# First half's attention in a hybrid encoder layer: vector work moved between a step's low halves and its normalisation, ScalarE's part moved to the step's head, one weight unit per step

## The chip, the cores and the metric

One core of one Trainium2 chip runs the whole layer as one program. The metric is the device time of one execution in microseconds (us). The engines are TensorE (PE in the profile; PEld is its loading of weights), VectorE (DVE), ScalarE (ACT), GpSimd (POOL) and the queue that issues most loads (SP). Each works through its own list of instructions in order, and they wait for one another through semaphores.

## The reference, cut to what matters

One layer over 1024 positions of width 1024. The change lies in branch B of the token mixer, a windowed attention with 8 query heads and 2 key/value heads of width 64, in blocks of 128 positions:

```python
q = rmsnorm(q.reshape(b, s, N_HEADS, HEAD_DIM), q_gain)
k = rmsnorm(k.reshape(b, s, N_KV_HEADS, HEAD_DIM), k_gain)
v = v.reshape(b, s, N_KV_HEADS, HEAD_DIM)
# each block of 128 queries sees its own block of keys and one on either side
logits = einsum('bnqkgd,bnskd->bnkgqs', qb, kb) * HEAD_DIM ** -0.5
logits = where(valid, logits - slope * distance, -1e30)
probs = softmax(concatenate([logits, sink_logit]))[..., :-1]
out = einsum('bnkgqs,bnskd->bnqkgd', probs, vb)
```

Beside it stand branch A (a gated mixing of 128 positions, with u and v from the same input projection), the sigmoid gates of both branches, an output projection and a gated feed-forward layer. All is float32; a product of two matrices is made of three passes over operands that are split into a high half and a low half (high x high, high x low, low x high).

## The kernel before, in words

The 1024 positions are done in two halves of 512 (`half(0)`, `half(1)`); each half has four query blocks i and two key/value heads kv. **A step** is one pair (i, kv), `work[s]`, so a half has steps 0 to 7. Step s does, in program order:

- `q_step(s)`, the *scores*: for four heads two matmuls each into a PSUM bank `at`, and on VectorE a custom instruction that adds the bias and takes the maximum (`lb`, `nmx`; ISA in an order's row, CUSTOM_DVE_ANT_0 in a profile's).
- `transposed(st)`: the probabilities of step s-1 (`lb`) are transposed on TensorE, block by block, and split: ScalarE casts the high half (`pH`), VectorE subtracts for the low half (`pL`).
- `exps`: VectorE makes `es`, ScalarE the exponentials of step s (`lb`) and of the sink (`es`).
- two *fillers*: 12 matmuls of another product (v of branch A first, then the gates), which give TensorE something to do.
- `normalise`: VectorE adds the sink, takes the reciprocal (`den`) and scales the four `lb`.
- `values`: TensorE multiplies the probabilities of step s-1 by `vt`; ScalarE copies half of the result (`xs`), VectorE adds the other half (`xs`), ScalarE casts it (`mid`), GpSimd subtracts for its low half.
- `beside(s)`, in the first half only: what the later steps need and was not ready before the loop: the split of the values (`v_split`, tiles `vt`), the split of the last query block (`q_halves(3)`, tiles `t`), its transposes (`q_turn(3)`), the norm and scale of the last key block (`k_norm(4)` with `kms` and `krs`; `k_put(4)` with `kd`) and its transposes (`turn_k`, into `kbuf`).
- one more filler.

In this stretch `in_order[0]` is true, so every engine's list has the order of the program text. There are four banks `at`, taken in turn: the scores take four, the transposes of a three-block step three, the values one. The scores of a step therefore take over banks that VectorE's `pL` and `xs` of the step before let go, and the first transposes of a step take over the bank of its first scores, which VectorE's custom instruction (`nmx`) lets go.

A *weight unit* is 128x1024 of a weight matrix: a load into `raw`, ScalarE's cast `wh`, and the subtraction `wl`, which `prepare` gives to GpSimd. `prepare_due` at a step's start makes as many units as the fillers have used up; before the change `beside(1)` makes one more, ahead of need.

Almost every instruction has line 76 in the profile (a helper records it), so groups are told apart by their tiles.

Of the kernel before, what the change touches and what calls it, by code (L numbers as in the profile page):

```python
# [38 lines left out]
def kernel(  # L39
# [709 lines left out]
    def half(hf):  # L749
# [323 lines left out]
        def begin_unit():  # L1073
            r = raw_unit(srcs.pop(0))
            h, l = (wpool.tile([P, UNIT], F32R, tag=x, name=nm(x)) for x in ("wh", "wl"))
            A.copy(h, r)
            units.append((h, l))
            return lambda: V.tensor_tensor(l, r, h.bitcast(F32), op=ALU.subtract)
# [109 lines left out]
        if hf == 0:  # L1188
# [92 lines left out]
            vgs = []  # L1281
            vr = sm(NT, "vr")

            def beside(s):
                if s == 0:
                    q_turn(2)
                    kv_tile(4, 0)
                    turn_k(2, 2)
                    kv_tile(4, 1)
                    k_evict(4)  # L1290
                    lows.append(begin_unit())
                elif s == 1:
                    q_halves(3)
                    v_split(2)
                    k_norm(4)
                    prepare()
                elif s == 2:
                    v_split(3)
                    q_turn(3)
                elif s == 3:  # L1300
                    v_split(4)
                    k_put(4)
                elif s == 4:
                    turn_k(4, 1)

            lows = []
        else:
            kraw, banks = [], []
            for b in range(3):
# [59 lines left out]
        for s in range(nw):  # L1369
            if s:  # L1370
                prepare_due()
                sc = q_step(s)
                if hf == 0 and s == 1:
                    lows.pop()()
                pts = transposed(st)
                den = exps(*sc, work[s][1])
            fill(FA if hf or s else 0)
            if hf == 0 and 0 < s < 7:
                x_square(s + 1)
            if hf == 0 and s == 7:  # L1380
                x_rstd()
            if hf == 0 and s == 5:
                load(silu_d, silu_c)
            normalise(sc[0], sc[2], den)
            if s == 0:
                end_unit()
            st = sc[0]
            if s == nw - 1:
                for vg in vgs:
                    act[0] = after(A.activation(vg, vg, AF.Gelu_apprx_tanh), act[0])  # L1390
                for t, vg in enumerate(vgs[:3]):
                    V.tensor_tensor_reduce(
                        out=stream("hs"), in0=vg, in1=vg, op0=ALU.mult, op1=ALU.add,
                        scale=1.0, scalar=0.0, accum_out=vr[:, t : t + 1])
            if s:
                i, kv = work[s - 1]
                values(base + i, koff, kv, pts, vts, i, oH, oL)
            if s == nw - 1:
                A.activation(stream("hs"), vgs[3], AF.Square, accum_out=vr[:, 3:])
                for vg in vgs[:2]:  # L1400
                    V.tensor_tensor(vg, vg, vgain, op=ALU.mult)
                V.tensor_scalar(vr, vr, 1.0 / GW, EPS, op0=ALU.mult, op1=ALU.add)
                G.tensor_tensor(vr, vr, nhalf[:, :NT], op=ALU.pow)
            if hf == 0:
                beside(s)
            fill(FB)
        pts = transposed(st)
        fill(FC)
# [55 lines left out]
            copies = {}  # L1464
        if hf == 0:
            ada_load()
            x_load(0)
            x_load(1)
            jobs.extend((k, lambda k=k: x_mod(k)) for k in range(KT))
# [12 lines left out]
        for d in range(KT):  # L1482
# [14 lines left out]
            for br, t in ((1, (oH, oL)), (0, (gH, gL))):  # L1497
# [4 lines left out]
                for k in range(4):  # L1502
                    kc = slice(br * Q + k * P, br * Q + (k + 1) * P)
                    mm3(pb, (wab[d][0][:, kc], wab[d][1][:, kc]), (t[0][:, k, :], t[1][:, k, :]),
                        k == 0, k == 3)
                if hf + d == 0 and br:
                    x_spread()
                if d < 2:
                    sg = gates.pop(0)
                    V.scalar_tensor_tensor(out=sg, in0=sg, scalar=1.0, in1=pb, op0=ALU.add,  # L1510
# [819 lines left out]
```

## Time and profile before

| | |
|---|---|
| median of 3 runs | 1236.48 us (1235.93 to 1240.13) |
| the profiled execution | 1236.45 us, of which the span of its instructions is 1234.6 us |
| TensorE (PE) busy | 1218.2 us, 99% of the span |
| VectorE (DVE) busy | 913.4 us, 74% |
| ScalarE (ACT) busy | 582.5 us, 47% |
| GpSimd (POOL) busy | 183.8 us, 15% |
| mean granted clock of TensorE | 0.997 |
| steps 1 to 7 of the first half | about 82.8 to 152.6 us of the span |

A timeline's row has the start, the time busy, the engine, the operation, the written and the read tiles with their sizes, the count of instructions put together, and in brackets the idle time before with what ended it. A row of windows has a stretch of the span, then the busy time of each engine in it, then the clock that TensorE was granted (1.00 is full), the busy share of the DMA engines, and GB/s. TensorE is pipelined and the ends of its matmuls are modelled, so the starts of rows are the better ruler.

### The profile page before, as it was taken

What the parts mean: (1) busy time and instruction counts of PE and PEld (TensorE: products, weight loads), DVE (VectorE), ACT (ScalarE), POOL (GpSimd) and SP (SyncE); (2) the same over time, 40 slices, a digit from 0 to 9 for tenths busy, and PEclk for the clock granted to TensorE, in tenths of its full rate; (3) what the DMA queues carried; (4) which work ended last, traced back from release to release, by engine and by line L of the source; (5) the groups of instructions that cost most, each with busy time, mean ns of one, the idle gap of its engine ahead of it and who ended that gap; (6) DMA issues with size and microseconds to landing.
All of it is one profiled execution on the core that took longest, in us unless ns stands there. A gap on an engine that the chain in (4) does not pass through costs nothing.

```text
span 1234.6 us, 15745 instructions
## 1 busy us (share of the span) xinstructions
PE 1218.2 (99%) x5680; PEld 1014.8 (82%) x5680; DVE 913.4 (74%) x1542; ACT 582.5 (47%) x954; POOL 183.8 (15%) x231
## 2 busy tenths in 40 slices
PE   8997999999999999999999999999999999999998
PEld 7886888888888887888888888888888888888887
DVE  9887786388898799877798666766766666666746
ACT  5586864267886333534553323333333334434342
POOL 0134331023342001222100000010000000010001
PEclk9998999999999999999999999999999999999999
DMA  9812249421147557877613445554555459996542
GB/s 346 322 52 69 78 148 323 161 86 53 59 140 257 176 180 255 284 269 243 234 35 120 140 151 204 187 208 155 212 194 188 170 187 372 337 351 235 188 171 102
DMA packets 78621, 235.76 MB, mean 191 GB/s; under 512 B 9344, under 2 KB 9680, under 8 KB 73552
## 3 DMA queue, kind: packets, MB, share of 16 engines
q1 hardware_dynamic: 56112, 141.43, 32.9%
q0 software_dynamic: 18976, 87.04, 19.8%
q10 hardware_dynamic: 3456, 6.29, 1.4%
q8 instruction: 44, 0.72, 0.2%
q14 instruction: 33, 0.27, 0.1%
HBM read 177.06 MB, written 57.67 MB: 190 GB/s over the span
## 4 chain that ended last, share of the span: by engine, by line
PE 90%; ACT 4%; DVE 3%; DMA 2%; issue 1%; SPq 0%; POOL 0%; DVEq 0%; ACTq 0%; POOLq 0%
PE at L76 46%; PE mm L76 45%; ACT lb L76 1%; ACT mid L76 1%; DVE lb L76 1%; ACT pH L76 1%; DMA mid<-in_xo_dram 1%; DMA raw<-in_w_ga_dram 0%; DVE xs L76 0%; DMA raw<-in_w_ada_dram 0%; DVE vt L76 0%; ACT wh L76 0%; SPq L137 0%; ACT t L76 0%; DVE t L76 0%
## 5 line engine op out<-in xcount | busy, mean ns | idle before, releaser
L76 ACT CAST wh<-raw 128x1024 fp32r<-128x1024 f32 (+1 forms) x156 | 161.7, 1039 | 142.2 <-PE mm L76 34.6
L76 DVE TENSOR_TENSOR wl<-raw,wh 128x1024 fp32r<-128x1024 f32 (+1 forms) x147 | 171.1, 1169 | 75.1 <-ACT wh L76 69.6
L76 PE MATMUL mm<-mid,wh 128*128 128x512 f32 x696 | 214.9, 390 | 0.0
L76 PEld LDWEIGHTS mm<-mid,wh 128*128 128x128 f32 x696 | 130.5, 188 | 27.0 <-DVE mid L76 0.2
L76 PE MATMUL at<-j,wh 128*128 128x512 f32 x464 | 142.9, 389 | 0.0
L76 PE MATMUL mm<-mid,wl 128*128 128x512 f32 x348 | 135.9, 390 | 0.6 <-DVE wl L76 0.6
L76 PE MATMUL mm<-wh,h 128*128 128x512 f32 x320 | 104.4, 398 | 0.5 <-ACT h L76 0.5
L76 PEld LDWEIGHTS at<-j,wh 128*128 128x128 f32 x464 | 87.1, 188 | 18.0
L76 DVE TENSOR_TENSOR wl<-ws,wh 128x1024 fp32r<-128x1024 f32 (+1 forms) x53 | 59.1, 1114 | 54.0 <-ACT wh L76 54.0
L76 PE MATMUL at<-j,wl 128*128 128x512 f32 x232 | 90.2, 389 | 0.0
L76 PE MATMUL mm<-j,wh 128*128 128x512 f32 x288 | 89.0, 390 | 0.0
L76 PE MATMUL mm<-h,wh 128*128 128x512 f32 x272 | 84.5, 392 | 0.0
L76 PE MATMUL at<-h,wh 128*128 128x512 f32 x272 | 84.3, 391 | 0.0
L76 PEld LDWEIGHTS mm<-mid,wl 128*128 128x128 f32 x348 | 65.3, 188 | 15.5 <-DVE wl L76 2.1
L76 ACT CAST wh<-ws 128x1024 fp32r<-128x1024 f32 (+1 forms) x53 | 50.9, 961 | 53.3 <-DVE ws L76 35.4
L76 PEld LDWEIGHTS mm<-wh,h 128*128 128x128 f32 x320 | 60.1, 190 | 12.8 <-ACT h L76 0.9
L76 PEld LDWEIGHTS mm<-j,wh 128*128 128x128 f32 x288 | 53.9, 188 | 11.1
L76 PEld LDWEIGHTS at<-h,wh 128*128 128x128 f32 x272 | 50.7, 188 | 11.2 <-DVE mid L76 0.8
L76 DVE TENSOR_TENSOR ol<-raw,oh 128x1024 fp32r<-128x1024 f32 x30 | 36.6, 1224 | 30.7 <-ACT oh L76 29.1
L76 PEld LDWEIGHTS mm<-h,wh 128*128 128x128 f32 x272 | 50.6, 188 | 10.3
L76 PE MATMUL mm<-wl,h 128*128 128x512 f32 x160 | 58.8, 392 | 0.0
L76 PE MATMUL mm<-j,wl 128*128 128x512 f32 x144 | 56.2, 390 | 0.0
(325 smaller groups left out, 2591.7 us busy)
## 6 DMA issues: line engine op xcount, KB each, us to landing
raw<-in_w_gate_dram SPq DMA_DIRECT2D x28, 512.0 KB, 5.2
tA<-hid POOLq DMA_DIRECT2D x11, 1024.0 KB, 5.0
tB<-hid POOLq DMA_DIRECT2D x11, 1024.0 KB, 5.5
wo<-in_w_out_dram POOLq DMA_DIRECT2D x22, 512.0 KB, 6.8
wS<-wo POOLq DMA_DIRECT2D x11, 1024.0 KB, 5.1
raw<-wS SPq DMA_DIRECT2D x44, 256.0 KB, 3.1
raw<-tB SPq DMA_DIRECT2D x44, 256.0 KB, 4.2
raw<-in_w_out_dram SPq DMA_DIRECT2D x33, 256.0 KB, 5.4
```

The source lines that it names most:

```text
L76: ins = f(*args, **kw)
```

## The change

`beside` is cut down to what TensorE does, and moves ahead of `values`. Three new places take the rest. `head(s)` stands behind the scores: ScalarE's casts of the values (`v_halves`) and of the query block (`q_begin`) are issued there, and VectorE's subtractions that belong to them are put on a list. `inside(s)` stands between `exps` and `normalise`: it runs that list (`run_lows`), and makes `k_norm(4)` in step 3 and `k_put(4)` in step 4. `head(5)` makes the weight unit that `beside(1)` made, so that each step from 2 on makes one. The query split moves from step 1 to step 3, its transposes from step 2 to step 4, and the transposes of the key block from step 4 to step 5. Apart from the attention, `x_spread` (four matmuls and a ScalarE copy that spread the next half's norm over the partitions) moves from between the first two output products to ahead of the loads of the next half's input.

```diff
+            def v_halves(t):
+                vts[t] = halo_v[t] = vt = attp.tile([P, 2, P], F32R, tag="vt", name=nm("vt"), bufs=5)
+                src = kraw(t)[:, P:]
+                for h in range(NKV):
+                    A.copy(vt[:, h, h * HD : (h + 1) * HD], src[:, h * HD : (h + 1) * HD])
+                    lows.append(lambda h=h: V.tensor_tensor(
+                        vt[:, h, (1 - h) * HD : (2 - h) * HD], src[:, h * HD : (h + 1) * HD],
+                        vt[:, h, h * HD : (h + 1) * HD].bitcast(F32), op=ALU.subtract))
+
+            def q_begin(t):
+                q3 = qraw[:, t, :].rearrange("p (h d) -> p h d", d=HD)
+                q0[t] = [tmp(F32R) for _ in range(2)]
+                for g in range(2):
+                    src = q3[:, g * 4 : g * 4 + 4, :]
+                    q4 = q0[t][g].rearrange("p (h a d) -> p h a d", a=2, d=HD)
+                    A.copy(q4[:, :, 0, :], src)
+                    lows.append(lambda q4=q4, src=src: V.tensor_tensor(
+                        q4[:, :, 1, :], src, q4[:, :, 0, :].bitcast(F32), op=ALU.subtract))
+
+            def head(s):
+                if s == 1:
+                    lows.append(begun.pop())
+                elif s == 2:
+                    v_halves(2)
+                    v_halves(3)
+                elif s == 3:
+                    q_begin(3)
+                elif s == 4:
+                    v_halves(4)
+                elif s == 5:
+                    prepare()
+
+            def run_lows():
+                while lows:
+                    lows.pop(0)()
+
+            def inside(s):
+                run_lows()
+                if s == 3:
+                    k_norm(4)
+                elif s == 4:
+                    k_put(4)
+
             def beside(s):
                 if s == 0:
                     q_turn(2)
...
-                    lows.append(begin_unit())
-                elif s == 1:
-                    q_halves(3)
-                    v_split(2)
-                    k_norm(4)
-                    prepare()
-                elif s == 2:
-                    v_split(3)
+                    begun.append(begin_unit())
+                elif s == 4:
                     q_turn(3)
-                elif s == 3:
-                    v_split(4)
-                    k_put(4)
-                elif s == 4:
+                elif s == 5:
                     turn_k(4, 1)
...
                 sc = q_step(s)
-                if hf == 0 and s == 1:
-                    lows.pop()()
+                if hf == 0:
+                    head(s)
+                    if s == 1:
+                        run_lows()
                 pts = transposed(st)
                 den = exps(*sc, work[s][1])
             fill(FA if hf or s else 0)
+            if hf == 0:
+                inside(s)
...
             st = sc[0]
+            if hf == 0:
+                beside(s)
...
-            if hf == 0:
-                beside(s)
             fill(FB)
...
         if hf == 0:
             ada_load()
+            x_spread()
             x_load(0)
             x_load(1)
...
-                if hf + d == 0 and br:
-                    x_spread()
```

**VectorE between step 1 and step 2.** The first rows are the list before, from the add of step 1's values (`xs`) to the first custom instruction of step 2's scores; `t` are the halves of the query block, `vt` the values, `kms` the key block's norm.

```order
L76 TENSOR_TENSOR xs_1057<-at_1052,xs_1057 64x512
L76 TENSOR_TENSOR t_167_1062<-mid_609,t_167_1062 128x4x64
L76 TENSOR_TENSOR t_168_1065<-mid_609,t_168_1065 128x4x64
L76 TENSOR_TENSOR vt_1068<-kraw_791,vt_1068 128x64 x2
L76 TENSOR_REDUCE kms_1073<-t_171_1074 128x2
L76 TENSOR_SCALAR kms_1073<-kms_1073 128x2
L76 ISA lb_1102,nmx_1098<-at_1099,bias,nsink 128x384
```

The same place in the changed kernel:

```order
L76 TENSOR_TENSOR xs_1057<-at_1052,xs_1057 64x512
L76 ISA lb_1078,nmx_1074<-at_1075,bias,nsink 128x384
L76 ISA nmx_1074 128x1
L76 ISA lb_1083,nmx_1074<-at_1080,bias,nsink 128x384
L76 ISA nmx_1074 128x1
```

Five rows that stood between the add and the scores of the next step are gone from there; so are, in the same way, the two `vt` rows between steps 2 and 3, and the `vt` and `kd` rows between steps 3 and 4.

**VectorE in step 3**, from the sink's exponent to the reciprocal. Before:

```order
L76 TENSOR_TENSOR pL_1251<-at_1245,pH_1250 128x512
L76 TENSOR_TENSOR es_1226<-rows,nmx_1205 128x4
L76 TENSOR_TENSOR den_1255<-den_1255,es_1226 128x4
L76 RECIPROCAL den_1255<-den_1255 128x4
L76 TENSOR_SCALAR lb_1209<-lb_1209,den_1255 128x384
```

and in the changed kernel:

```order
L76 TENSOR_TENSOR pL_1224<-at_1218,pH_1223 128x512
L76 TENSOR_TENSOR es_1195<-rows,nmx_1174 128x4
L76 TENSOR_TENSOR t_205_1196<-mid_609,t_205_1196 128x4x64
L76 TENSOR_TENSOR t_206_1197<-mid_609,t_206_1197 128x4x64
L76 TENSOR_REDUCE kms_1248<-t_218_1249 128x2
L76 TENSOR_SCALAR kms_1248<-kms_1248 128x2
L76 TENSOR_TENSOR den_1228<-den_1228,es_1195 128x4
L76 RECIPROCAL den_1228<-den_1228 128x4
L76 TENSOR_SCALAR lb_1178<-lb_1178,den_1228 128x384
```

The query's subtractions and the key block's norm now stand between `es` and `den`; `kms` reads a square that ScalarE makes behind the exponentials of this step.

**ScalarE in step 5**, from the last exponential to the copy of the values (`t` are the evictions of branch A's v, `hs` the square for the next half's norm, `kbuf` the key block's high half). Before:

```order
L76 ACTIVATE es_1439<-es_1439 128x4
L76 COPY t_278_1480<-mm_846 128x512
L76 COPY t_279_1482<-mm_847 128x512
L76 ACTIVATE hs_1491,xms_443<-hs_1491 128x512
L76 COPY xs_1508<-at_1501 64x512
```

and in the changed kernel:

```order
L76 ACTIVATE es_1428<-es_1428 128x4
L76 COPY t_277_1475<-mm_846 128x512
L76 COPY t_278_1477<-mm_847 128x512
L76 ACTIVATE hs_1486,xms_443<-hs_1486 128x512
L76 CAST kbuf<-at_1496 128x2x128
L76 COPY xs_1508<-at_1501 64x512
```

The cast into `kbuf`, which the scores of step 6 read, moved from step 4 to here, behind two evictions and a square.

More of the change, by code (lines that the diff above doesn't have):

```diff
@@ L1290, in beside @@
                     k_evict(4)
-                    lows.append(begin_unit())
-                elif s == 1:
-                    q_halves(3)
-                    v_split(2)
-                    k_norm(4)
-                    prepare()
-                elif s == 2:
-                    v_split(3)
+                    begun.append(begin_unit())
+                elif s == 4:
                     q_turn(3)
-                elif s == 3:
-                    v_split(4)
-                    k_put(4)
-                elif s == 4:
+                elif s == 5:
                     turn_k(4, 1)
-            lows = []
+            lows, begun = [], []
         else:
```

## The prediction

> **What bounds the kernel now.** I read the page's busy times first, then TensorE's waits in the attention stretch.
>
> ```profile
> span 1234.6 us, 15745 instructions
> PE 1218.2 (99%) x5680; PEld 1014.8 (82%) x5680; DVE 913.4 (74%) x1542; ACT 582.5 (47%) x954; POOL 183.8 (15%) x231
> PE at L76 <- DVE nmx L76: 7.8, 3, 4.5
> ```
>
> TensorE bounds the span; only the 16.4 us in which it idles (1234.6 - 1218.2), and time in which it runs slowly, can be had. The last row is its longest kind of wait from 80 to 160 us (in sum, times, longest): half of all its idle time. Next, its timeline, where a row `at<-kbuf` starts a step's scores and `at<-ident,lb` its transposes:
>
> ```profile
> 89.76 1.55 PE L76 MATMUL at<-kbuf,mid 128*128 128x384 f32 x8
> 93.77 1.97 PE L76 MATMUL at<-ident,lb 128*128 128x128 f32 x8 [2.46 <-DVE nmx L76]
> 101.93 0.85 PE L76 MATMUL at<-kbuf,mid 128*128 128x384 f32 x4
> 103.12 0.62 PE L76 MATMUL at<-kbuf,mid 128*128 128x384 f32 x2 [0.33 <-ACT mid L76]
> 104.52 0.62 PE L76 MATMUL at<-kbuf,mid 128*128 128x384 f32 x2 [0.78 <-DVE nmx L76]
> 104.98 1.47 PE L76 MATMUL at<-ident,lb 128*128 128x128 f32 x12
> 111.80 1.55 PE L76 MATMUL at<-kbuf,mid 128*128 128x384 f32 x8
> 117.87 2.82 PE L76 MATMUL at<-ident,lb 128*128 128x128 f32 x12 [4.53 <-DVE nmx L76]
> 126.38 1.20 PE L76 MATMUL at<-kbuf,mid 128*128 128x384 f32 x6
> 128.01 0.62 PE L76 MATMUL at<-kbuf,mid 128*128 128x384 f32 x2 [0.43 <-DVE kbuf L76]
> 135.66 1.55 PE L76 MATMUL at<-kbuf,mid 128*128 128x384 f32 x8
> 144.17 1.56 PE L76 MATMUL at<-kbuf,mid 128*128 128x384 f32 x8
> 152.55 1.47 PE L76 MATMUL at<-ident,lb 128*128 128x128 f32 x12
> ```
>
> Steps 2 to 7 start at 89.76, 101.93, 111.80, 126.38, 135.66 and 144.17, and end at 152.55. They last 12.17, 9.87, 14.58, 9.28, 8.51 and 8.38 us. Step 7 is clean, and 8.38 is my measure of a step's TensorE work. Why the slow steps lose more than their waits is in the granted clock (behind the five busy times):
>
> ```profile
> 93.70:97.10 3.40, 3.33 (x13) 3.00 (x14) 3.03 (x11) 1.91 (x5) 3.40 (x3) 0.53 0.00 0
> 104.50:107.00 2.50, 2.48 (x18) 2.31 (x19) 2.35 (x8) 1.38 (x3) 2.37 (x1) 1.00 0.00 0
> 117.80:121.10 3.30, 3.23 (x15) 3.15 (x15) 2.87 (x10) 1.48 (x3) 0.00 (x0) 0.55 0.02 5
> ```
>
> After the waits of 2.46 and 4.53 TensorE ran at half speed for 3.4 and 3.3 us, which lost (1 - 0.53) x 3.4 = 1.6 and (1 - 0.55) x 3.3 = 1.5. After 0.33 and 0.78 close together it kept 1.00.
>
> What VectorE was at while TensorE waited for `nmx`:
>
> ```profile
> 89.22 0.68 DVE L76 TENSOR_TENSOR xs<-at,xs 64x512 f32<-64x512 f32 x1
> 90.89 1.63 DVE L76 TENSOR_TENSOR t<-mid,t 128x256 fp32r<-128x256 f32 x2 [0.99 <-ACT t L76]
> 93.10 0.61 DVE L76 CUSTOM_DVE_ANT_0 lb<-at,bias,nsink 128x384 f32<-128x384 f32 x1
> 109.71 0.16 DVE L76 TENSOR_TENSOR den<-den,es 128x4 f32<-128x4 f32 x1 [1.52 <-ACT es L76]
> 113.08 3.55 DVE L76 TENSOR_TENSOR vt<-t,vt 128x64 fp32r<-128x64 f32 x2 [0.83 <-ACT vt L76]
> 116.55 0.47 DVE L76 SCALAR_TENSOR_TENSOR kd<-t,krs,gqk 128x64 f32<-128x64 f32 x2
> 114.21 2.34 POOL L76 TENSOR_TENSOR wl<-raw,wh 128x1024 fp32r<-128x1024 f32 x1
> ```
>
> The scores of step 2 were in PSUM from about 90.1, and VectorE came to them at 93.10, through the query's subtractions. Step 4's scores it held up to about 117.2, with `kd` and with two `vt` subtractions that took 3.55 us: the second could only go when GpSimd's weight subtraction ended (114.21 + 2.34 = 116.55). Yet a little earlier it idled 1.52 us ahead of `den`, waiting for ScalarE.
>
> **The change part by part.** I count a step's excess over its own work.
>
> ```profile
> 106.21 0.48 PE L76 MATMUL mm<-wh,h 128*128 128x512 f32 x1
> ```
>
> Twelve transposes take 1.23 us (104.98 to 106.21), 0.10 each, and the 24 matmuls of 128x512 from 106.21 to the scores at 111.80 take 0.23 each. Step 2 has 4 transposes and 2 value matmuls fewer than step 7, and 8 turns of the query more, at 0.10: 8.38 - 0.41 - 0.46 + 0.8 = 8.3. Step 4 has two turns of the key more, 0.2 at most: 8.5.
>
> Excess: step 2, 12.17 - 8.3 = 3.9; step 3, 9.87 - 8.38 = 1.5; step 4, 14.58 - 8.5 = 6.1; step 5, 0.9; step 6, 0.1; together 12.5 us, clock included. The turns only change their step, so TensorE's work remains.
>
> *Removed from ahead of the scores.* Step 2 loses its five rows between `xs` and the first `lb`: VectorE is free at 89.9 and the scores are there at 90.1, so the first transposes (due at 91.2, when the scores are through TensorE) wait for nothing: 3.9 us gained, 1.6 of it clock. In step 3 the `vt` go and so do the turned query's evictions that held two banks: 1.5 gained. In step 4 `vt` and `kd` go: 6.1 gained, if nothing new comes. The 0.9 of step 5 belongs to `kbuf`, which moves on.
>
> *Added between `es` and `den`.* The gap there was 1.5 us. Into it go: step 2, four `vt`, whose pair took 0.35 undisturbed (0.7); step 3, two `t`, together 1.63 at most; step 4, two `vt`, two `kd` and a copy (0.35 + 0.47 + some 0.2). All fit but for 0.1, and are costed at nothing; without the gap they would cost these 0.7 to 1.6. But `k_norm` doesn't fit: its `kms` needs a ScalarE square that stands behind the exponentials. The rows for this, for its chain, and for the rest of ScalarE's list (the first is a piece of the chain of waits, the last a row of windows over a step):
>
> ```profile
> 147.92 2.40 ACT lb L76 x8
> 92.45 0.35 DVE L76 TENSOR_TENSOR vt<-kraw,vt 128x64 fp32r<-128x64 f32 x2
> 91.37 0.30 ACT L76 ACTIVATE t<-t 128x128 f32<-128x128 f32 x1
> 92.72 0.27 DVE L76 TENSOR_REDUCE kms<-t 128x2 f32<-128x128 f32 x1
> 90.46 0.71 ACT L76 CAST t<-mid 128x256 fp32r<-128x256 f32 x2
> 110.12 1.41 DVE L76 TENSOR_SCALAR lb<-lb,den 128x384 f32<-128x384 f32 x4
> 127.13 0.37 ACT L76 CAST kbuf<-at 128x256 fp32r<-128x256 f32 x1
> 133.49 1.05 ACT L76 COPY t<-mm 128x512 f32<-128x512 f32 x2
> 134.44 0.63 ACT L76 ACTIVATE hs<-hs 128x512 f32<-128x512 f32 x1
> 138.11 1.57 ACT L76 CAST pH<-at 128x512 fp32r<-128x512 f32 x3
> 135.00:143.50 8.50, 8.50 (x46) 7.06 (x45) 6.67 (x20) 7.44 (x20) 3.64 (x2) 1.00 0.17 57
> ```
>
> *New wait at step 4's transposes.* In step 6 before, with a weight cast ahead, `pH` started 1.0 us behind the transposes (138.11; the scores took 1.42 from 135.66, as 8 x 0.18, so transposes from 137.1). The query's casts of 0.7 at step 3's head make that 1.7; `pH` 1.6, exponentials 2.4 and `es` 0.1 end 5.8 behind the transposes' start. From there: square 0.3; reduction 0.27 and a scaling like `den`'s 0.16; `den` and reciprocal 0.4 (109.71 to 110.12); `lb` 1.4; `xs` 0.7; the first custom instruction 0.6: 3.8, so the bank is free at 9.6. TensorE, through transposes (1.2), 12 + 6 + 6 matmuls (5.6) and the scores (1.4), is there at 8.2. **New wait: 1.4 us.** VectorE is late, with `lb`, `xs` and the scores queued behind `kms`.
>
> *New wait at step 6's scores.* In step 5's head ScalarE has two evictions (1.05) and the weight cast ahead of `pH`, which starts 1.0 + 1.05 behind the transposes and brings `es` at 6.1; then evictions 1.05, square 0.6 and `kbuf` 0.37 end at 8.2, where TensorE, after transposes, 24 matmuls and turns, wants it at 7.0. **New wait: 1.2 us**, and some 0.2 for the low half.
>
> *Weight unit and spread.* With one unit a step, the second `v` unit is made at step 2's head and read by that step's last filler, 6.1 us behind the scores' start (8.3 less the turns' 0.8 and its own 1.4). ScalarE's cast follows `mid`, about 0.8 behind that start; cast 1.0 and subtraction 2.3 end at 4.1, or at 4.9 behind the subtraction of the values, so it costs nothing; without that cover it would cost up to its 2.3. Loads are issued units ahead. `x_spread` costs its four matmuls in either place, but VectorE's list behind it starts earlier, which can take this later wait:
>
> ```profile
> 183.73 0.50 PE L76 MATMUL mm<-mid,wl 128*128 128x512 f32 x1 [0.34 <-DVE wl L76]
> ```
>
>
> Sum: 12.5 gained, 1.4 + 1.2 + 0.2 given back: 9.7, and 0.2 from the spread: 1236.45 - 9.9 = 1226.55, say **1226.5 us**. The sum is made against the profiled execution's own 1236.45, of which 1234.6 is span; the median is 1236.48. Bounds of the new waits: nothing, if ScalarE is ahead of TensorE after all (1236.45 - 12.7 = 1223.7), and 2.2 us each if GpSimd's root (`krs`, right behind `kms`) or a late subtraction holds VectorE for up to another 0.8 (1228.1). I take the sum's, since its terms are rows of the same instructions.
>
> **The rivals.**
>
> *The clock falls again.* The two new waits lie between 0.78 + 0.33, which left the clock at 1.00, and 2.46, which halved it. Each halving adds 1.6: 1228.1 or 1229.7. For it: neither length has been seen in a stretch that was busy before. Against: both are nearer to the harmless pair (1.1 in 1.6 us).
> [...]
>
> *The inserted work waits for GpSimd.* As in 113.08's row, a `vt` or `t` that meets a weight subtraction sits out its 2.3 us, and each step from 2 on now has one such unit. In four steps the gap of 1.5 hides all but 0.8: 3.3 lost, 1229.8. Against: the weight cast stands first in ScalarE's list, so GpSimd should end before `es`.
> [...]
>
> *ScalarE becomes the bound: slower.* It was busy 7.44 us in the stretch of step 6, and step 5 now has that list and 2.1 of evictions and 0.4 of `kbuf` on top: 9.9, over TensorE's 8.4. If each of steps 2 to 6 came 2.4 late by it and so halved the clock, 5 x 4.0 = 20 would stand against 12.5: 1236.45 + 7.5 = 1243.9. It decides from some 2.4 us of lateness a step; against it, only step 5's sum is over at all, and steps 2 to 4 add 0.3 to 1.3 to theirs.
>
> *The gain is given back later*, in the loads from 170 to 200 us:
>
> ```profile
> 190.00:200.00 10.00, 10.00 (x46) 8.28 (x45) 5.80 (x8) 5.06 (x8) 2.17 (x4) 1.00 0.97 354
> ```
>
> The DMA engines are 97% busy there; if half the gain ended in them, 1231.5. Against: the loads follow freed buffers and shift along, and TensorE doesn't wait there.
>
> **How the numbers follow.** Forecast 67%, clock 15%, GpSimd 7%, given back 6%, slower 3%; 2% that TensorE only waits for the next thing in the same places, near 1236. I take 0.5% (6.2 us) as what a measurement of this kernel can tell from no change. Faster by more, below 1230.3: the first three, 0.89. Same: given back and the same waits, 0.08. Slower: 0.03. The range runs from 1223.7, no new wait, to 1230.1, just over the clock's and GpSimd's cases, and leaves out the rest.
>
> **What would show it.** In the changed profile the `nmx` waits of 2.46 and 4.53 are gone and the clock stays 1.00 from 89 to 125 us; the scores of step 3 start near 97; TensorE waits about 1.4 us at step 4's transposes or last scores, behind `xs` and `nmx`, and 1.2 at step 6's scores for `kbuf`; the last transposes start near 142.9. A clock of 0.5 there, a `vt` of 2 us, or TensorE idle from 170 on would prove the forecast wrong.

## The result, and the profile after

The changed kernel takes **1225.47 us** (median of 4 runs, 1224.65 to 1228.35) against 1236.2 for the kernel before, run beside it. The ratio is 0.991, with a 95% interval of 0.9884 to 0.9937. A second set of four runs gave 1227.34 us and 0.9921 (0.9906 to 0.9936). The change makes the kernel about 0.9% faster; 1226.5 was predicted, with a range of 1223.7 to 1230.1.

The profiled execution took 1226.18 us. Its span and busy times on the page:

```profile
span 1224.1 us, 15741 instructions
PE 1215.7 (99%) x5680; PEld 1013.2 (83%) x5680; DVE 906.4 (74%) x1542; ACT 582.5 (48%) x954; POOL 183.6 (15%) x231
```

The span is 10.5 us shorter. TensorE's idle time fell from 16.4 us to 8.4 (1224.1 - 1215.7), and its busy time, with the same 5680 matmuls, by 2.5 (1218.2 - 1215.7). The matmuls at half speed are part of those 2.5; how large a part was not measured. TensorE's waits from 80 to 160 us (in sum, times, longest) no longer have a row for `nmx` under PE, where two rows are left; its loads of weights (PEld) still wait for `nmx`, 0.4 at the longest where it was 4.8, and twice for `xs`, 1.0 in sum:

```profile
PE at L76 <- ACT kbuf L76: 0.4, 1, 0.4
PE at L76 <- DVE xs L76: 0.4, 1, 0.4
PEld at L76 <- DVE nmx L76: 0.8, 3, 0.4
```

The timeline of TensorE, with the starts of scores (`at<-kbuf`) and transposes (`at<-ident,lb`), and two windows whose column behind the five busy times is the granted clock:

```profile
89.72 1.55 PE L76 MATMUL at<-kbuf,mid 128*128 128x384 f32 x8
97.04 1.83 PE L76 MATMUL at<-kbuf,mid 128*128 128x384 f32 x8
98.92 1.73 PE L76 MATMUL at<-ident,lb 128*128 128x128 f32 x12
106.01 1.20 PE L76 MATMUL at<-kbuf,mid 128*128 128x384 f32 x6
107.57 0.61 PE L76 MATMUL at<-kbuf,mid 128*128 128x384 f32 x2 [0.36 <-DVE xs L76]
108.11 1.73 PE L76 MATMUL at<-ident,lb 128*128 128x128 f32 x12
115.90 1.56 PE L76 MATMUL at<-kbuf,mid 128*128 128x384 f32 x8
117.30 1.57 PE L76 MATMUL at<-ident,lb 128*128 128x128 f32 x12
124.22 0.40 PE L76 MATMUL mm<-h,wl 128*128 128x512 f32 x1
125.04 1.94 PE L76 MATMUL at<-kbuf,mid 128*128 128x384 f32 x8 [0.42 <-ACT kbuf L76]
126.90 1.73 PE L76 MATMUL at<-ident,lb 128*128 128x128 f32 x12
142.37 1.47 PE L76 MATMUL at<-ident,lb 128*128 128x128 f32 x12
```

```profile
89.00:125.00 36.00, 35.21 (x184) 28.80 (x183) 28.67 (x89) 31.25 (x83) 15.38 (x9) 1.00 0.34 117
170.00:200.00 30.00, 30.00 (x134) 24.86 (x133) 20.64 (x28) 14.85 (x21) 4.31 (x8) 1.00 0.94 337
```

Steps 2 to 7 now start at 89.72, 97.04, 106.01, 115.90, 125.04 and 133.99, and step 7 ends at 142.37. In the stretch of the attention the clock is 1.00 throughout, and from 170 to 200 us TensorE is busy in all 30 us. Step lengths in us, in the profiles before and after:

| | step 2 | 3 | 4 | 5 | 6 | 7 | sum |
|---|---|---|---|---|---|---|---|
| before | 12.17 | 9.87 | 14.58 | 9.28 | 8.51 | 8.38 | 62.79 |
| after | 7.32 | 8.97 | 9.89 | 9.14 | 8.95 | 8.38 | 52.65 |

The sum is 10.14 us shorter; the rest of the span behind step 7 is 1082.05 before and 1081.73 after. So the time came from the steps, and nothing was given back behind them.

What now stands on VectorE between `es` and `den`, and where ScalarE and GpSimd come in (timelines of the changed kernel, in steps 2, 3, 4 and 5):

```profile
91.83 2.41 POOL L76 TENSOR_TENSOR wl<-raw,wh 128x1024 fp32r<-128x1024 f32 x1
93.89 0.38 DVE L76 TENSOR_TENSOR es<-rows,nmx 128x4 f32<-128x4 f32 x1
94.19 0.62 DVE L76 TENSOR_TENSOR vt<-kraw,vt 128x64 fp32r<-128x64 f32 x4
95.66 0.16 DVE L76 TENSOR_TENSOR den<-den,es 128x4 f32<-128x4 f32 x1 [0.85 <-ACT es L76]
100.44 1.55 ACT L76 CAST pH<-at 128x512 fp32r<-128x512 f32 x3
102.92 0.76 DVE L76 TENSOR_TENSOR t<-mid,t 128x256 fp32r<-128x256 f32 x2
104.29 0.20 ACT L76 ACTIVATE es<-es 128x4 f32<-128x4 f32 x1
104.72 0.29 DVE L76 TENSOR_REDUCE kms<-t 128x2 f32<-128x128 f32 x1 [1.04 <-ACT t L76]
107.44 0.60 DVE L76 CUSTOM_DVE_ANT_0 lb<-at,bias,nsink 128x384 f32<-128x384 f32 x1
111.93 0.36 DVE L76 TENSOR_TENSOR vt<-t,vt 128x64 fp32r<-128x64 f32 x2
113.52 0.16 DVE L76 TENSOR_TENSOR den<-den,es 128x4 f32<-128x4 f32 x1 [0.58 <-ACT es L76]
123.18 0.16 DVE L76 TENSOR_TENSOR den<-den,es 128x4 f32<-128x4 f32 x1 [1.41 <-ACT es L76]
124.61 0.38 ACT L76 CAST kbuf<-at 128x256 fp32r<-128x256 f32 x1
```

In steps 2 and 4 `den` still waits for ScalarE behind the inserted work (0.85 and 0.58), so that work cost VectorE nothing there. The two `vt` that had taken 3.55 us take 0.36. In step 3 VectorE waits 1.04 for the square ahead of `kms`, as the prediction feared.

### The profile page after: what moved, and what is told of

Same layout as the page of the kernel before. It is cut to its first block, busy times and chain, and to the rows that moved or that the text cites. A ratio compares the mean times of both kernels' runs of the same rounds, so it can differ in the third digit from the quotient of the medians.

```text
span 1224.1 us, 15741 instructions
## 1 busy us (share of the span) xinstructions
PE 1215.7 (99%) x5680; PEld 1013.2 (83%) x5680; DVE 906.4 (74%) x1542; ACT 582.5 (48%) x954; POOL 183.6 (15%) x231
## 4 chain that ended last, share of the span: by engine, by line
PE 85%; DMA 5%; DVE 5%; ACT 3%; issue 1%; POOL 0%; SPq 0%; DVEq 0%; ACTq 0%; POOLq 0%
PE at L76 43%; PE mm L76 43%; DMA raw<-tA 2%; DMA raw<-in_w_ga_dram 1%; DVE wl L76 1%; ACT wh L76 1%; DVE mid L76 1%; DVE hs L76 1%; DMA mid<-in_w_ada_dram 1%; ACT lb L76 1%; DVE raw L76 1%; DMA mid<-in_xo_dram 1%; DVE t L76 0%; DMA hs<-md 0%; DVE lb L76 0%
## 5 line engine op out<-in xcount | busy, mean ns | idle before, releaser
L76 PEld LDWEIGHTS at<-h,wh 128*128 128x128 f32 x272 | 50.9, 188 | 10.5
```

Of the source, the lines that this page charges most:

```text
L76: ins = f(*args, **kw)
```

## The experiments

Runs of one kernel scatter by 1 to 6 us, so step lengths from the profiles are the finer ruler, and the times are the check. All ratios are to the kernel before, run beside each, with 95% intervals. In the table the sum is that of steps 2 to 7.

| kernel | 2 | 3 | 4 | 5 | 6 | 7 | sum |
|---|---|---|---|---|---|---|---|
| before, with zeros in two waits | 10.84 | 14.15 | 13.49 | 9.35 | 8.54 | 8.39 | 64.76 |
| the same with one unit a step | 10.85 | 10.33 | 13.34 | 9.38 | 8.42 | 8.37 | 60.69 |
| before, step 3's part moved | 12.32 | 9.70 | 8.54 | 9.68 | 8.53 | 8.37 | 57.14 |
| after, step 3's part back | 7.30 | 8.99 | 16.29 | 8.85 | 8.97 | 8.36 | 58.76 |
| before, unit and spread alone | 12.35 | 9.72 | 14.68 | 9.15 | 8.47 | 8.37 | 62.74 |
| before, step 4's unit late | 12.24 | 9.80 | 11.23 | 12.92 | 8.33 | 8.33 | 62.85 |
| after, two units in step 1 | 7.32 | 10.40 | 9.90 | 8.53 | 8.62 | 8.37 | 53.14 |
| after, casts behind the exponentials | 7.33 | 9.37 | 10.05 | 9.59 | 8.95 | 8.38 | 53.67 |
| after, key block a step earlier | 7.30 | 10.65 | 9.01 | 8.33 | 9.23 | 8.38 | 52.90 |
| after, both waits shortened | 7.30 | 8.99 | 9.51 | 8.54 | 9.20 | 8.33 | 51.87 |
| after, again | 7.28 | 9.04 | 9.91 | 9.14 | 8.95 | 8.40 | 52.72 |

**Half of the change at a time.** First the kernel before with only step 3's part moved into step 4; then its complement, the changed kernel with that part put back behind the values of step 3.

```diff
 # on the kernel before
-                elif s == 3:
-                    v_split(4)
-                    k_put(4)
...
+                if hf == 0 and s == 4:
+                    v_halves(4)          # behind the scores
...
+            if hf == 0 and s == 4:       # between es and den
+                while vlows:
+                    vlows.pop(0)()
+                k_put(4)
 # the complement, on the changed kernel
-                elif s == 4:
-                    v_halves(4)
...
-                elif s == 4:
-                    k_put(4)
...
+            if hf == 0 and s == 3:       # behind the values
+                v_split(4)
+                k_put(4)
```

> The kernel before, with only the third value split (casts at step 4's head, subtractions behind es) and the key scale moved from the end of step 3 to ahead of den in step 4. Theory (VectorE's own order makes each wait): step 4 loses its 4.53 us wait and the half clock behind it, 6.1 us, while step 2 keeps its 2.46; the key's scale now comes later, so step 5's wait for kbuf may grow from 0.43 to about 1: 1236.4 - 6.1 + 0.5 = 1230.8 us. Rival (the waits hang together: a step that comes earlier only runs into the next one): under 3 us gained, 1233.5 or more.

> The changed kernel, with only step 3's part undone: the third value split and the key's scale stand behind the values of step 3 again. It is the complement of the kernel that had that part alone (step 4 6.0 us shorter, step 5 0.4 longer, 5.1 us in the times). Theory (each wait is made by what stands ahead of its own scores, so the parts add up): step 4's wait is back, 3 to 4.5 us with the clock fallen behind it, steps 2 and 3 stay as short as in the changed kernel: the sum from step 2's scores is 52.65 + 5 to 6, the time about 1231.5 us. Rival (one part is enough to keep the chain in pace): within 3 us of the changed kernel.

Measured: 1231.22 us, ratio 0.9959 (0.9941 to 0.9976), and 1231.02 us, ratio 0.9957 (0.9943 to 0.9971), both as expected in the times; the complement's sum is 6.11 above the changed kernel's, where 5 to 6 were expected. In the complement the old wait stands in step 4 in full. Its timelines of VectorE and TensorE, and a window behind the wait, with the clock at 0.50:

```profile
107.86 3.56 DVE L76 TENSOR_TENSOR vt<-t,vt 128x64 fp32r<-128x64 f32 x2 [0.83 <-ACT vt L76]
112.66 2.82 PE L76 MATMUL at<-ident,lb 128*128 128x128 f32 x12 [4.95 <-DVE nmx L76]
```

```profile
112.40:115.80 3.40, 3.14 (x14) 3.05 (x15) 2.97 (x10) 1.40 (x3) 0.00 (x0) 0.50 0.02 5
```

The first saves 5.65 us of the six steps (62.79 - 57.14), the complement 4.03, together 9.68 of the whole change's 10.14. The parts add up: each part's place decides in its own step. Both parts move VectorE's subtractions and ScalarE's casts together; the casts' place alone is worth 1.0 (below), so most of it is VectorE's. The move of `beside` ahead of `values` was not tested by itself.

**The clock by itself.** The kernel before, with matmuls of zeros added to a bank of branch A's v where TensorE had waited 2.46 and 4.53 us. They keep TensorE running, leave the order of the other engines as it is, and change no value.

```diff
+                if hf == 0 and s in (2, 4):
+                    still(vps[3:] * (10 if s == 2 else 19))
```

> The kernel before, with 10 matmuls of zeros between the scores and the transposes of step 2 and 19 in step 4, added into an open accumulator that they leave as it is: TensorE has 2.3 and 4.4 us of idle work in its two long waits, and VectorE's order is unchanged. Theory (the waits cost their length and then 1.6 and 1.5 us of half clock): the clock stays at 1.00 in both places, steps 2 and 4 are 1.6 and 1.5 us shorter, the whole about 1233.3 us. Rival (the slow matmuls behind the waits are late for another reason, such as banks or operands that come late): no change, 1236.4, and the matmuls behind the zeros are as slow as before.

Measured: 1234.96 us, ratio 0.9987 (0.9974 to 0.9999): less than expected. The clock stayed 1.00 behind both filled waits, and steps 2 and 4 got shorter by 1.33 and 1.09 us. But in the profiled execution step 3 grew by 4.28. This kernel's timelines of GpSimd, VectorE and TensorE, and two windows:

```profile
94.22 4.77 POOL L76 TENSOR_TENSOR wl<-raw,wh 128x1024 fp32r<-128x1024 f32 x2
96.73 2.28 DVE L76 TENSOR_TENSOR es<-rows,nmx 128x4 f32<-128x4 f32 x1
101.88 0.62 PE L76 MATMUL at<-kbuf,mid 128*128 128x384 f32 x2 [0.50 <-DVE xs L76]
103.43 0.62 PE L76 MATMUL at<-kbuf,mid 128*128 128x384 f32 x2 [0.93 <-ACT mid L76]
104.81 1.01 PE L76 MATMUL at<-kbuf,mid 128*128 128x384 f32 x2 [0.77 <-DVE nmx L76]
```

```profile
100.80:104.20 3.40, 1.82 (x7) 0.81 (x6) 2.38 (x5) 2.32 (x6) 1.27 (x1) 1.00 0.23 77
105.60:109.00 3.40, 3.40 (x15) 3.22 (x14) 2.25 (x6) 1.70 (x4) 1.70 (x1) 0.50 0.00 0
```

GpSimd's two weight units, one right behind the other, held VectorE's `es` (a 128x4 subtraction, 2.28 us in place of 0.15) until they ended at 98.99. ScalarE had waited 0.76 for it when it came to the sink's exponential; `den`, `lb` and the values' `xs` and `mid` were late behind that, TensorE met them 1.3 us earlier than before, and after three short waits (0.50 + 0.93 + 0.77) the clock fell there instead. This was not so in every execution: the mean granted clock was 0.997 in this one and one other, and 0.999 or 1.000 in the remaining eight of the ten. The reading of `es` was then tested: the same kernel with the second unit moved from step 1 to step 5.

```diff
                     k_norm(4)
-                    prepare()
...
                     still(vps[3:] * (10 if s == 2 else 19))
+                if hf == 0 and s == 5:
+                    prepare()
```

> The kernel before with the zeros in the waits of steps 2 and 4, and in addition one unit per step (the unit of step 1's end at step 5's head). In the kernel with the zeros alone the clock stayed full in step 2, and yet step 3's transposes came no earlier, since es of step 2 sat out GpSimd's two subtractions (2.28 us) and TensorE idled 0.50 + 0.93 + 0.77 in step 3's scores. Theory (that pair of units is what hid the gain of the clock): es now ends about 2.3 us earlier, den 0.7 to 1 earlier, step 3's transposes start 0.7 to 1 nearer to step 2's, the idle in step 3's scores is under 1.6 and the clock stays at 1.00: the sum from step 2's scores about 61 us (62.79 before, 64.75 with the zeros alone). Rival (the chain through ScalarE and the query's evictions sets step 3 whatever GpSimd does): step 3's transposes as late as with the zeros alone, within 0.3, and the idle 2 us.

Measured: 1233.28 us, ratio 0.9974 (0.9965 to 0.9983), sum of steps 60.69. `es` takes 0.15 us, step 3's scores wait 0.82 + 0.77, the clock stays 1.00, and step 3 is 10.33. So the pair of units made `es` late, and the waits behind which the clock had fallen were shorter without it. The clock alone is then worth 2.1 us of the steps (62.79 - 60.69), in an execution whose mean clock was 1.000, as in six of the ten: 1.24 in step 4, and 0.86 in steps 2 and 3 together.

**The weight unit and the spread.** Alone on the kernel before, and, the other way round, the changed kernel with the unit back in step 1.

```diff
 # on the kernel before
-                    prepare()            # step 1, behind k_norm
+                if hf == 0 and s == 5:
+                    prepare()            # behind the scores
...
             ada_load()
+            x_spread()
...
-                if hf + d == 0 and br:
-                    x_spread()
 # on the changed kernel
-                elif s == 5:
-                    prepare()
...
+            if hf == 0 and s == 1:
+                prepare()
             fill(FB)
```

> The kernel before, with only the two smaller parts of the change: the weight unit of step 1's end goes to step 5's head, and the spread of the norm ahead of the loads of the next half's input. Theory (they carry almost nothing): 1236.4 - 0.3 = 1236.1 us, all three long waits as before. Rival (GpSimd's two units in a row hold VectorE in step 2, and the unit is a cause of the waits): step 2's or step 4's wait shrinks by over 1 us, 1235 or less.

> The changed kernel, with one weight unit per step undone: the unit of step 5's head is made at the end of step 1 again, so that GpSimd has two subtractions in a row in step 2 and none in step 5's head. Theory (a VectorE instruction with both inputs in SBUF waits for a GpSimd subtraction in flight, and the unit matters once the other work is out of the way): es of step 2 waits until about 96.6 on the clock of the changed kernel's profile, was 94.3, den comes about 1.5 us later, steps 2 and 3 together 1 to 1.5 us longer; step 5's head is lighter by a cast of 1.0, so the wait for kbuf at step 6's scores goes and steps 5 and 6 together are 0.6 to 1 shorter. In sum 0 to 0.9 longer from step 2's scores to the last transposes (52.65 in the changed kernel). Rival (the unit's place has no part in it): step 2's es isn't late, steps 2 and 3 as in the changed kernel within 0.2.

Measured: alone 1235.38 us, ratio 0.9989 (0.9979 to 0.9998), with every step within 0.2 us of the kernel before: all but nothing. In the changed kernel 1225.6 us, ratio 0.9912 (0.9898 to 0.9927), and 0.49 us more in the steps. Timelines of GpSimd, VectorE and TensorE with two units:

```profile
91.15 4.79 POOL L76 TENSOR_TENSOR wl<-raw,wh 128x1024 fp32r<-128x1024 f32 x2
94.16 1.81 DVE L76 TENSOR_TENSOR es<-rows,nmx 128x4 f32<-128x4 f32 x1
99.02 0.61 PE L76 MATMUL at<-kbuf,mid 128*128 128x384 f32 x2 [1.45 <-DVE xs L76]
```

The 0.49 is a difference of two larger numbers. Steps 2 and 3 are 1.43 longer, since `es` is held again; steps 5 and 6 are 0.94 shorter, because step 5 has no weight cast ahead of `pH` and `kbuf` comes in time. The unit is worth something only once the vector work is out of the way or the long waits are filled, as with the zeros.

**The unit alone, moved behind the exponentials.** The kernel before with step 4's unit made late, so that the two `vt` ahead of the scores don't meet it.

```diff
-                prepare_due()
+                if hf or s != 4:
+                    prepare_due()
                 sc = q_step(s)
...
                 den = exps(*sc, work[s][1])
+                if hf == 0 and s == 4:
+                    prepare_due()
```

> The kernel before, with only step 4's weight unit issued behind the exponentials of that step, no longer ahead of its scores, so that GpSimd's subtraction doesn't run when the value split does. Theory of the port (of the 3.55 us of the two vt subtractions all but 0.35 is waiting for GpSimd, 2.3 of it for the weight unit, the rest for the subtraction of the values): vt takes about 1.2 to 1.3 us, step 4's wait falls from 4.53 to about 2.2, the clock still falls: 1236.4 - 2.3 = 1234.1 us. Rival (the subtractions are slow of themselves or wait for ScalarE): vt stays over 3 us, 1236.4.

Measured: 1235.51 us, ratio 0.9995 (0.9983 to 1.0008): no gain, against the expectation. This kernel's timelines of VectorE, TensorE and GpSimd, and two windows, one behind each wait:

```profile
112.64 1.38 DVE L76 TENSOR_TENSOR vt<-t,vt 128x64 fp32r<-128x64 f32 x2 [0.83 <-ACT vt L76]
115.26 1.73 PE L76 MATMUL at<-ident,lb 128*128 128x128 f32 x12 [2.35 <-DVE nmx L76]
120.61 3.55 DVE L76 TENSOR_SCALAR lb<-lb,den 128x384 f32<-128x384 f32 x4
121.18 2.44 POOL L76 TENSOR_TENSOR wl<-raw,wh 128x1024 fp32r<-128x1024 f32 x1 [7.38 <-ACT wh L76]
124.94 0.62 PE L76 MATMUL at<-kbuf,mid 128*128 128x384 f32 x2 [1.49 <-DVE xs L76]
126.44 0.62 PE L76 MATMUL at<-kbuf,mid 128*128 128x384 f32 x2 [0.88 <-DVE kbuf L76]
```

```profile
115.20:118.60 3.40, 3.34 (x20) 2.79 (x21) 3.40 (x11) 2.59 (x6) 0.00 (x0) 1.00 0.05 13
126.90:130.30 3.40, 3.40 (x16) 3.06 (x16) 3.05 (x11) 1.81 (x5) 1.09 (x2) 0.56 0.06 23
```

That `vt` waits for GpSimd's subtraction was right as far as it went: `vt` fell from 3.55 to 1.38 us, the wait from 4.53 to 2.35, and step 4 is 3.35 us shorter; the clock, which was expected to fall here, held. But the subtraction now met VectorE's scaling: the four `lb` took 3.55 us, where they had taken 1.41. `xs` was late behind it, the scores of step 5 waited 1.49 + 0.88, the clock fell there, and step 5 is 3.64 us longer in this execution, whose mean clock was 0.997. In five of the ten it was 0.999, so the length of step 5 is not the same in all of them. The collision was moved and not removed. The rows show the two engines' times beside each other and not what they share, so the port of the theory's name is not shown.

**ScalarE's place at the head.** The changed kernel with ScalarE's casts behind the exponentials, the subtractions staying between `es` and `den`.

```diff
             def head(s):
...
-                elif s == 2:
-                    v_halves(2)
-                    v_halves(3)
-                elif s == 3:
-                    q_begin(3)
-                elif s == 4:
-                    v_halves(4)
...
             def inside(s):
+                if s == 2:
+                    v_halves(2)
+                    v_halves(3)
+                elif s == 3:
+                    q_begin(3)
+                elif s == 4:
+                    v_halves(4)
                 run_lows()
```

> The changed kernel, with ScalarE's part at the head undone: the casts of the values and of the query are issued behind the exponentials of the step, right ahead of the subtractions that need them. Theory (the casts belong at the head, since den would wait for es, cast and subtraction one after the other): in steps 2, 3 and 4 den comes later by the casts (0.6, 0.7, 0.3) and the subtractions (0.6, 0.8, 0.3), less what the exponentials start earlier (0.3 to 0.7): steps 3 to 5 together 1 to 3 us longer, 1226.5 to 1228.5 us, waits at the scores or first transposes for xs and nmx over 1 us. Rival (only VectorE's place of the subtractions matters): the same as the changed kernel, 1225.5 within 0.5 by the step lengths.

Measured: 1225.99 us, ratio 0.9915 (0.99 to 0.993). In the times it can't be told from the changed kernel; the steps are 53.67, 1.0 more (two profiles of the changed kernel differ by 0.07). The place at the head is worth that 1.0, the least of the 1 to 3 that were expected, and no wait at the scores is over 1 us: TensorE's two for `xs` make 0.9 together.

**The key block a step earlier.** The changed kernel with the square at the head of step 2, the norm in step 2, `k_put` and the key's transposes in step 3; it asks whether the two waits left can be had by moving the chain.

```diff
                     v_halves(3)
+                    k_norm_begin(4)      # square on ScalarE; norm and root go on the list
...
                 if s == 3:
-                    k_norm(4)
-                elif s == 4:
                     k_put(4)
...
-                elif s == 4:
-                    q_turn(3)
-                elif s == 5:
+                elif s == 3:
                     turn_k(4, 1)
+                elif s == 4:
+                    q_turn(3)
```

> The changed kernel, with the last key block's work earlier: its square at the head of step 2, reduction behind step 2's value subtractions, scale in step 3, turns at the end of step 3. Theory (the changed kernel's remaining waits are den behind the square in step 3, and kbuf behind ScalarE's evictions at step 6's scores): both waits (0.36 and 0.42) go, step 3's chain is 0.7 shorter and step 6's scores start 0.6 to 1 earlier; steps 3 to 6 lose about 1.2 of their 2.5 us of excess: 1224.3 us. Rival (ScalarE's list is what bounds steps 3 to 6 now, so a piece moved to another step costs there what it saves here): 1225.5, steps 2 to 6 in sum within 0.4 us of the changed kernel.

Measured: 1225.95 us, ratio 0.9921 (0.9897 to 0.9946), steps 52.90. The sum is the rival's, within its 0.4: the cost moves. Steps 4 and 5 are 0.9 and 0.8 us shorter, but step 6 is 0.3 longer, and step 3 is 1.7 longer, since TensorE reaches the key's transposes before `kd` is made. That wait is for VectorE, so it doesn't show that ScalarE's list is the bound, as the rival had it:

```profile
104.97 0.44 PE L76 MATMUL at<-ident,kd 128*128 128x128 f32 x2 [0.99 <-DVE kd L76]
```

**Both waits shortened in place.** The changed kernel with only the key's square at the head of step 3, and with two of the v evictions given to VectorE between `es` and `den` of step 5, where it had idled 1.41 us.

```diff
                     q_begin(3)
+                    k_norm_begin(4)
...
-                if s == 3:
-                    k_norm(4)
-                elif s == 4:
+                if s == 4:
                     k_put(4)
...
-                    A.copy(vgs[t], vps[t])
+                    (V.tensor_copy if t > 1 else A.copy)(vgs[t], vps[t])
```

> The changed kernel, with both of its new waits taken at their cause: the key's square moves from behind step 3's exponentials to step 3's head, so that den follows es at once, and two of the four evictions of branch A's v in step 5 go from ScalarE to VectorE, into its idle stretch between es and den. Theory (den is late by the square, kbuf by the evictions): step 4's last scores no longer wait (0.36), step 6's scores start about 0.6 to 1 earlier, 51.2 to 51.8 from step 2's scores to the last transposes against 52.65; about 1224.5 us, too little for the times to tell. Rival (another instruction is late next to it, such as ScalarE's casts at the head): 52.4 or more.

Measured: **1223.22 us** (1222.89 to 1224.0), ratio 0.9894 (0.9879 to 0.9909), the fastest here: it beats the kernel before clearly, and the changed kernel by about 0.8 us in the steps (51.87 against 52.65 and 52.72); the intervals of the two ratios overlap. From 51.2 to 51.8 were expected. Timelines of VectorE and TensorE:

```profile
102.90 0.28 DVE L76 TENSOR_REDUCE kms<-t 128x2 f32<-128x128 f32 x1
103.83 0.17 DVE L76 TENSOR_TENSOR den<-den,es 128x4 f32<-128x4 f32 x1 [0.44 <-ACT es L76]
124.11 1.49 PE L76 MATMUL at<-kbuf,mid 128*128 128x384 f32 x7 [0.61 <-DVE kbuf L76]
```

VectorE no longer waits ahead of `kms`, and `den` waits for ScalarE again. What is left is VectorE's half of `kbuf`, which stands behind the four scalings; it took back 0.25 of the 0.6 gained in step 5.

## Why the prediction was right, by its own steps

**The waits ahead of the scores are gone: right.** Step 2 was to last 7.5 us (8.3 less the 0.8 of the query's turns) and lasts 7.32. The scores of step 3 start at 97.04 for the 97 predicted, the clock is 1.00 from 89 to 125, and the `vt` took 0.36. Step 3 was to be clean at 8.38 and is 8.97. So of the 1.5 to be gained there, 0.9 came. From its scores to its transposes 1.88 us pass, where step 5 takes 1.40: the last scores' bank came late from `xs`, which the prediction didn't count, since it never added up step 2's chain as it did those of steps 3 and 5. Two rows of the changed kernel, on ScalarE and on VectorE:

```profile
91.35 0.68 ACT L76 CAST vt<-kraw 128x64 fp32r<-128x64 f32 x4
97.51 0.69 DVE L76 TENSOR_TENSOR xs<-at,xs 64x512 f32<-64x512 f32 x1
```

The four casts at the head stand ahead of `pH`, which starts 0.95 behind the transposes (91.11 to 92.06). The sink's exponential ends at 95.62, and the chain behind it brings `xs` to its end at 98.20. The load for the last scores waits 0.33 for it, and the load for the transposes 0.36 for `nmx`. With two units in step 1, where `es` is held, the wait for `xs` at the same place is 1.45, so it is this chain that sets it. Whether the casts alone make it late was not tested.

**New wait at step 4: the mechanism right, the size too large.** Predicted 1.4 us. From the scores' start to the transposes it is 2.10 against 1.40, so 0.7, of which 0.36 is shown as a wait for `xs`. The terms, counted from the transposes of step 3 at 98.92: `pH` starts 1.52 behind (1.7 predicted), `es` ends at 5.57 (5.8), the chain from there to the end of the first custom instruction takes 3.55 (3.8), and TensorE is there at 8.49 (8.2). Three errors of 0.2 to 0.3 (up to `es`, with `pH` in it; the chain; TensorE's arrival) had the same sign and make up the 0.7 to 0.8 that was predicted too much. The subtractions were hidden, and the one that didn't fit, `k_norm`, was the one named. The last experiment removed its wait, and step 4 got 0.38 shorter; the other 0.3 is still there, with `den` waiting for ScalarE.

**New wait at step 6: right, a little too large.** Predicted 1.2 + 0.2. The filler's last matmul starts at 124.22 and its successor would follow 0.23 later; the scores start at 125.04, 0.6 late, and take 1.86 to the transposes in place of 1.40: 1.05 in all. `kbuf` ends 7.7 behind the transposes of step 5 (8.2 predicted).

**The sum.** Predicted 12.5 gained and 2.8 given back in the steps, 9.7; measured 10.14. The prediction's lengths without a wait add up to 50.3 (8.3 + 8.5 + 4 x 8.38), so 2.3 were given back: 0.6 in step 3, 0.7 in step 4, 1.05 at step 6's scores, less 0.2 in step 2, which is 2.15; 0.15 is left in the lengths themselves, which are good to no better. That the sum came so near is partly luck: the 0.6 overlooked in step 3 stood against 0.7 too much in step 4 and 0.35 at step 6. The 0.2 credited to the spread isn't settled: its wait of 0.34 for `wl` is gone, but the span behind step 7 differs by 0.3 between these two profiles and by up to 2.2 among the other kernels', so it can't be told. From profile to profile 9.9 were predicted and 10.27 measured (1236.45 - 1226.18).

**Three steps of the working that the runs correct.** First, "3.9 us gained, 1.6 of it clock" made the clock of step 2 a loss of its own. With the clock held, steps 2 and 3 gain 0.86 together; in step 4 the 1.5 is 1.24. The total was right since the changed kernel removes the wait and the slow time in one. Second, "so it costs nothing" on the weight unit: the prediction had put its cast into step 5's sum, and 0.94 of steps 5 and 6 is the price of that; but it takes 1.43 out of steps 2 and 3, which was not seen, though the kernel before shows VectorE held by the two units there (its timeline of VectorE):

```profile
97.01 1.69 DVE L76 TENSOR_TENSOR es<-rows,nmx 128x4 f32<-128x4 f32 x1
```

Third, ScalarE's casts at the head were treated as a cost alone; the later place costs 1.0 more.

**The rivals.** The clock didn't fall: the two new waits show as 0.4 each (0.7 and 0.6 by the starts) and not as 1.2 to 1.4, so the case that the prediction had doubted was not reached. GpSimd held none of the inserted work. It held `es` a little in steps 2 and 5 (0.38 and 0.24 us in place of 0.15), where `den` had to wait for ScalarE in any case. ScalarE didn't become the bound, and the loads took nothing back. That the first two are real mechanisms and were near is what the zeros and the late unit show: in both, GpSimd's subtraction held VectorE (`es` 2.28 us, the four `lb` 3.55), TensorE's waits added up (to 2.20 and 2.37), and in the profiled execution the clock fell (to 0.50 and 0.56).

## What to carry to other kernels

In an engine's list that is worked in order, look for a place where the engine waits for a partner anyway (here `es` to `den`, 1.5 us a step): work put there cost next to nothing, except for the one instruction that waited for ScalarE itself, and the same work ahead of the instruction that lets a bank go had cost TensorE some 10 us. Move the partner's share ahead as well, and check what ends last at the new place, since that is where the next wait appears. Here a collision between two engines was only solved where the slow instruction came to lie beside work that it doesn't block (the last two `vt` take 0.36 us in place of 3.55, and the custom instructions beside GpSimd keep their 0.6); moving it in time alone found the next victim (the four `lb`, 3.55 in place of 1.41).

## What the runs showed of the hardware that was not expected

**When the clock falls.** In the profiled executions it was 0.50 behind waits of 0.50 + 0.93 + 0.77 us (the zeros), with TensorE busy for 1.82 of 3.40 us, and 0.56 behind 1.49 + 0.88 (the late unit). It stayed at 1.00 behind single waits of 2.35 (the late unit) and 1.45 (two units in step 1), and behind 0.82 + 0.77 (the zeros with one unit a step), though behind a single 2.46 in the kernel before it was 0.53. Neither the longest wait nor their sum alone orders these: 2.35 in one piece kept it, 2.37 in two pieces (1.49 + 0.88) didn't. What does decide stays open. One kernel's executions differ in it, too: at half speed 3.4 us take 0.0014 off an execution's mean clock (1.7 of 1235 us), and with the zeros that mean was 0.997 in two executions and 0.999 or 1.000 in eight. So a fall in one profile doesn't say that the kernel has it each time; the kernel before had 0.995 to 0.997 in all its runs beside the kernels of the experiments, the changed one 1.000 in all eight. With the zeros no wait ahead of the fall was longer than 0.93.

**What a GpSimd subtraction holds.** Beside GpSimd's subtractions, of 2.4 us each for 128x1024, VectorE's 128x4 `es` took up to 2.28 us in place of 0.15 (two in a row), two `vt` of 128x64 3.55 in place of 0.36, and four scalings `lb` 3.55 in place of 1.41. The custom instructions and `pL`, which read PSUM, kept their 0.6 each beside it (0.61, and 1.28 for two `pL`, beside the two units with the zeros). The 128x4 instruction was held about as long as larger ones: 2.13 us, against 2.14 for the four `lb` and 3.19 for the two `vt`, which met two subtractions. What it costs depends on who waits: of the 2.28 us of `es`, ScalarE waited for 0.76, and what follows waits for ScalarE. In the profiles before and after, 18 `es` began while a `wl` or `mid` of GpSimd's was under way; each took 0.15 to 1.69 us and ended 0.02 to 0.13 behind it. Those held (`es`, `vt`, `lb`) read SBUF alone; what decides which instructions are held, no view here shows.
